# Loads of 16 heads in 16 KB runs, PSUM left in two copies, doubled mixes and transposes in a batched product x·yᵀ on one core

## The chip, the core and the metric

The kernel runs on one core of a Trainium2 chip. Its time is the device time of one launch in microseconds (us). Ten runs of the kernel before have a median of 302.0 us, from 301.79 to 302.33.

## The reference

For each of 8 batches and 12 heads, x and y are 512 x 64 matrices of float32, and the output is their product over the 64 channels, a 512 x 512 matrix of float32:

```python
batch, n_heads, seq_t, seq_s, channels = 8, 12, 512, 512, 64
np.einsum('bhtc,bhsc->bhts', x, y).astype(np.float32)
```

The inputs are 12.6 MB each, the output is 100.7 MB: for each byte read, four are written.

## The kernel before

All 96 heads are taken as one row of heads. A **group** is 8 heads (G); there are 12 (NG). `load` (L73) takes a group's x and y with two DMAs, 1 MB each, into one slot: on each of the 128 partitions 32 consecutive rows of x (8 KB) and 32 of y (8 KB). One pool of five slots of 16 KB per partition (`slots`, L54) serves loads and output tiles alike: an output tile is a slot as well, and `result` fills it before it is stored.

`compress` (L79) empties a slot of inputs: ScalarE casts x to bf16 (`xk`, L83), and the casts of y into `yb` are split in four quarters of 64 partitions: two on VectorE, one on GpSimd, one on ScalarE (`in_front`, L61; the instructions have the line of the helper `copy`, L66 for ScalarE, L68 for the others).

A **pair** `i` is four heads, half a group. `mix` (L99) copies four blocks of 32 partitions of `xk` into a tile `xb` of u32 words, in which one of the two bf16 places of a word stays zero for each half of the channels; two such tiles, one for even and one for odd pairs, are set to zero once (L148 to L150). `transposes` (L113) lets VectorE transpose `xb` and `yb` in blocks of 32 x 32 words into `xT` and `yT`. After that two heads lie one above the other on the 128 partitions of `xT`, with zeros that separate them, and so one matmul with 128 contraction rows makes 64 rows of each of two heads.

`result` (L126) makes output tile `o`, 2 MB: eight matmuls of 128 x 512, into PSUM tiles of 3, 3 and 2 banks (two buffers of 3 banks, one of 2), each copied to the slot by ScalarE, or by VectorE for each fourth tile. Behind that it emits, for later pairs, the transposes or the mixes (VectorE's and ScalarE's in turn). There are 48 output tiles, each stored in 16 KB runs.

The order on each engine is that of the program (`manual_schedule`, L145); engines wait for one another through semaphores alone. All DMAs are issued by SP, in program order, on one queue. The program goes like this: five loads, the zeros, and then for each group `compress`, half of a `mix` by GpSimd, and (L155 to L162) for groups 2 and 4 transposes, for groups 0 to 4 the next load, for groups 5, 7 and 9 an output tile into a slot that is held back, for groups 6 and 8 loads 10 and 11. The three tiles held back are stored after the last load (L163), and then 45 more tiles follow, each made and stored (L165). GpSimd makes the mixes of pairs 0 to 5 in this loop; the later ones come out of `result`.

On ScalarE's queue, for instance, result 0 stands between the casts of groups 5 and 6, result 1 between those of 7 and 8, result 2 between those of 9 and 10. SP issues load 10 when all casts of group 6 have read its slot, and load 11 when those of group 8 have.

Of the kernel before, what the change touches and what calls it, by code (L numbers as in the profile page):

```python
# [1 line left out]

# [4 lines left out]


@with_exitstack
def kernel(  # L10
    ctx: ExitStack,
    tc: tile.TileContext,
    x: bass.AP,
    y: bass.AP,
    out: bass.AP,
):

    nc = tc.nc
    B, H, T, C = x.shape
    _, _, S, _ = y.shape  # L30
    P = 128
    G = 8
    Q = P // G
    R = T // Q
    NG = B * H // G
    K = 8
    E = R // K
    D = 32
    SLOTS = 5
    fp32 = mybir.dt.float32  # L40
    bf16 = mybir.dt.bfloat16
    u32 = mybir.dt.uint32
    COPY = mybir.ActivationFunctionType.Copy
    assert C == 2 * D and S == T and R == D and Q * 2 == D

    xv = x.rearrange("b h t c -> (b h t c)").rearrange("(g p n) -> g p n", p=P, n=R * C)
    yv = y.rearrange("b h t c -> (b h t c)").rearrange("(g p n) -> g p n", p=P, n=R * C)
    ov = out.rearrange("b h t s -> (b h t s)").rearrange(
        "(o u h q n) -> o h q u n", u=2, h=2, q=Q * E, n=K * S
    )  # L50

    const = ctx.enter_context(tc.tile_pool(name="const", bufs=1))
    kept = ctx.enter_context(tc.tile_pool(name="kept", bufs=NG))
    slots = ctx.enter_context(tc.tile_pool(name="slots", bufs=SLOTS))  # L54
    tpool = ctx.enter_context(tc.tile_pool(name="tpool", bufs=3))
    pm3pool = ctx.enter_context(tc.tile_pool(name="pm3psum", bufs=2, space=bass.MemoryType.PSUM))
    pm2pool = ctx.enter_context(tc.tile_pool(name="pm2psum", bufs=1, space=bass.MemoryType.PSUM))

    loaded, inputs, mixed, made = {}, {}, {}, {}
    zeroed = [const.tile([P, K * E * D], u32, name=f"xb{half}") for half in range(2)]  # L60
    in_front = [nc.vector, nc.gpsimd, nc.vector, nc.scalar]  # L61
    FIRST = NG // 2

    def copy(engine, dst, src):
        if engine is nc.scalar:
            nc.scalar.activation(dst, src, COPY)  # L66
        else:
            engine.tensor_copy(dst, src)  # L68

    def slot():  # L70
        return slots.tile([P, K * S], fp32, name="slot")

    def load(g):  # L73
        both = slot()
        nc.sync.dma_start(both[:, :R * C], xv[g])
        nc.sync.dma_start(both[:, R * C:], yv[g])
        loaded[g] = both

    def compress(g):  # L79

        both = loaded.pop(g)
        xk = kept.tile([P, R, C], bf16)
        nc.scalar.activation(xk.rearrange("p r c -> p (r c)"), both[:, :R * C], COPY)  # L83
        inputs[g] = xk
        ys = both[:, R * C:].rearrange("p (r c) -> p r c", c=C)
        for half in range(2):
            yb = kept.tile([P, R // 2 * D], u32, name=f"yb{half}")
            yv2 = yb.bitcast(bf16).rearrange("p (j c w) -> p j w c", j=R // 2, w=2)
            for ch in range(2):
                copy(  # L90
                    in_front[2 * half + ch],
                    yv2[ch * 64:(ch + 1) * 64],
                    ys[half * 64:(half + 1) * 64, :, ch * D:(ch + 1) * D].rearrange(
                        "p (j w) c -> p j w c", w=2
                    ),
                )
            mixed[2 * g + half] = yb

    def mix(i, engines, halves=(0, 1)):  # L99

        g, half = divmod(i, 2)
        xk = inputs[g]
        xv2 = zeroed[half].bitcast(bf16).rearrange("p (k e c u) -> p k e c u", k=K, e=E, u=2)
        for ch in halves:
            for u in range(2):
                lo = half * 64 + u * D
                copy(
                    engines[2 * ch + u],
                    xv2[(2 * ch + u) * D:(2 * ch + u + 1) * D, :, :, :, u],
                    xk[lo:lo + D, :, ch * D:(ch + 1) * D].rearrange("p (e k) c -> p k e c", k=K),  # L110
                )

    def transposes(i):  # L113
        xb, yb = zeroed[i % 2], mixed.pop(i)
        xT = tpool.tile([P, K * D * E], u32)
        nc.vector.transpose(  # L116
            xT.rearrange("p (k r e) -> p k e r", k=K, e=E),
            xb.rearrange("p (k e c) -> p k e c", k=K, e=E),
        )
        yT = tpool.tile([P, D * R // 2], u32)  # L120
        nc.vector.transpose(  # L121
            yT.rearrange("p (r j) -> p j r", r=D), yb.rearrange("p (j c) -> p j c", c=D)
        )
        made[i] = (xT.bitcast(bf16).rearrange("p (k h m) -> p k h m", k=K, h=2), yT.bitcast(bf16))

    def result(o):  # L126

        i, h = divmod(o, 2)
        xT, yT = made[i]
        otf = slot()  # L130
        ot = otf.rearrange("p (r s) -> p r s", s=S)
        for k, n in ((0, 3), (3, 3), (6, 2)):
            pm = (pm3pool if n == 3 else pm2pool).tile([P, n, S], fp32, name=f"pm{n}")
            for j in range(n):
                nc.tensor.matmul(  # L135
                    pm[:, j, :], xT[:, k + j, h, :], yT[:, h * S:(h + 1) * S], start=True, stop=True
                )
            copy(nc.vector if o % 4 == 3 else nc.scalar, ot[:, k:k + n, :], pm)
        if h == 0 and i + 2 < 2 * NG:
            transposes(i + 2)  # L140
        elif h == 1 and FIRST <= i + 4 < 2 * NG:
            mix(i + 4, [nc.scalar if o % 4 == 3 else nc.vector] * 4)
        return lambda: nc.sync.dma_start(ov[i, h], otf)

    with tc.manual_schedule():  # L145
        for g in range(SLOTS):
            load(g)
        for k in range(0, K * E * D, 64):  # L148
            nc.vector.memset(zeroed[0][:, k:k + 64], 0.0)  # L149
            nc.gpsimd.memset(zeroed[1][:, k:k + 64], 0.0)  # L150
        stores = []
        for g in range(NG):
            compress(g)
            mix(g // 2, [nc.gpsimd] * 4, (g % 2,))
            if g in (2, 4):  # L155
                transposes(g // 2 - 1)
            if g < 5:
                load(g + SLOTS)
            elif g in (5, 7, 9):
                stores.append(result(len(stores)))  # L160
            elif g in (6, 8):
                load(g // 2 + 7)  # L162
        for store in stores:  # L163
            store()
        for o in range(len(stores), 4 * NG):  # L165
            result(o)()


# [1 line left out]
_INS = ['x', 'y']  # L170
_OUTS = [((8, 12, 512, 512), 'float32')]


# [23 lines left out]
```

## Time and profile before

| | us |
|---|---|
| median of 10 runs | 302.0 |
| the profiled execution | 301.86 |
| its span, from the first instruction to the last | 300.1 |
| TensorE matmuls busy | 144.5 |
| VectorE busy | 182.6 |
| ScalarE busy | 221.3 |
| GpSimd busy | 59.1 |

The groups of instructions that matter here, as the page lists them (busy us, count, mean ns of one):

| | busy | count | mean ns |
|---|---|---|---|
| ScalarE, PSUM to slot, 1536 elements | 100.8 | 72 | 1452 |
| ScalarE, PSUM to slot, 1024 elements | 37.3 | 36 | 1036 |
| VectorE, PSUM to slot, 1536 elements | 41.0 | 24 | 1751 |
| VectorE, PSUM to slot, 1024 elements | 14.6 | 12 | 1213 |
| VectorE transposes of xb / of yb | 49.1 / 25.3 | 24 / 24 | 2044 / 1056 |
| mixes: GpSimd / ScalarE / VectorE | 38.5 / 48.1 / 26.1 | 24 / 36 / 36 | 1606 / 1336 / 724 |
| y casts: VectorE / GpSimd / ScalarE | 33.8 / 19.2 / 15.9 | 24 / 12 / 12 | 1408 / 1602 / 1328 |
| x casts, ScalarE | 22.9 | 12 | 1910 |

How to read the page: PE is TensorE, DVE VectorE, ACT ScalarE, POOL GpSimd, and SPq the queue of SyncE. The DMA row cuts the span into 40 equal slices of 7.5 us; each digit is the mean busy share of the 16 transfer engines in tenths, 9 for 90% or more. In a timeline a line is: start, duration, engine, line of the code, operation, output and input with their shapes, count; in brackets, how long the engine had been idle before and what ended that. Several like instructions in a row are merged in one line, with the shape of the first. An issue of a DMA shows only the issuing; a transfer's landing is seen in the instruction that it releases.

### The profile page before, as it was taken

The page shows a single profiled execution, that of the slowest core. Times are in us where ns is not written, and L with a number is a line of the kernel's source. Part 1 is how long each engine was busy: PE and PEld are TensorE (multiplying, and loading weights), DVE is VectorE, ACT ScalarE, POOL GpSimd, SP SyncE. Part 2 cuts the span into 40 slices and gives each one's busy share as a digit, 9 for nine tenths or more (in the row PEclk, how much of TensorE's full clock was granted, in tenths as well). Part 3 has the DMA queues.
Part 4 walks back from the last instruction along what each step waited for, and adds up shares of the span by engine and source line. Part 5 has one row for each costly group of instructions (what it writes and reads, how often), then busy time and mean ns, then how long its engine had stood idle before and what let it go on. Part 6 is the DMA issues. An engine that isn't in the chain of part 4 may idle for free.

```text
span 300.1 us, 1419 instructions
## 1 busy us (share of the span) xinstructions
PE 144.5 (48%) x384; PEld 45.9 (15%) x384; DVE 182.6 (61%) x160; ACT 221.3 (74%) x169; POOL 59.1 (20%) x56
## 2 busy tenths in 40 slices
PE   0004044138646465765456657566585557574000
PEld 0001011012212121221112112112121112121000
DVE  1568895979983973937909649288295570603200
ACT  4666599998999869789789697897887977364000
POOL 2899999981000000000000000000000000000000
PEclk9999555557989776677986775857757895776555
DMA  7999999999999999999999999999999999999994
GB/s 289 429 425 422 419 419 426 423 436 431 424 436 430 421 439 430 426 435 430 427 439 426 432 430 428 432 435 426 430 435 428 422 425 435 423 424 430 430 430 210
DMA packets 10377, 125.93 MB, mean 420 GB/s; under 512 B 1152, under 2 KB 1152, under 8 KB 1152
## 3 DMA queue, kind: packets, MB, share of 16 engines
q1 hardware_dynamic: 10368, 125.83, 98.8%
q8 instruction: 3, 0.05, 0.1%
q14 instruction: 6, 0.05, 0.0%
HBM read 25.17 MB, written 100.66 MB: 419 GB/s over the span
## 4 chain that ended last, share of the span: by engine, by line
DMA 53%; ACT 11%; DVE 7%; issue 1%; DVEq 1%; PE 0%; ACTq 0%
DMA out_dram<-slot 53%; ACT slot L66 8%; DVE slot L68 7%; ACT xb L66 2%; ACT xk L83 1%; DVEq L192 1%; PE pm L135 0%; ACT yb L66 0%; DVE yb L68 0%; DVEq L68 0%; ACTq L66 0%
## 5 line engine op out<-in xcount | busy, mean ns | idle before, releaser
L135 PE MATMUL pm<-yT,xT 128*128 128x512 bf16 x384 | 144.5, 514 | 130.7 <-ACT slot L66 75.7
L66 ACT ACTIVATE slot<-pm 128x1536 f32<-128x1536 f32 (+1 forms) x108 | 133.2, 1314 | 37.9 <-DMA out_dram<-slot 28.8
L68 DVE COPY slot<-pm 128x1536 f32<-128x1536 f32 (+1 forms) x36 | 54.6, 1572 | 72.7 <-DMA out_dram<-slot 44.5
L135 PEld LDWEIGHTS <-xT 128*128 128x128 bf16 x384 | 45.9, 120 | 228.4 <-issue 193.4
L116 DVE STREAM_TRANSPOSE xT<-xb 128x1024 uint32<-128x1024 uint32 x24 | 49.1, 2044 | 5.6 <-PE pm L135 4.0
L66 ACT ACTIVATE xb<-xk 32x1024 bf16<-32x1024 bf16 x36 | 48.1, 1336 | 0.9
L68 DVE CAST yb<-slot 64x1024 bf16<-64x1024 f32 x24 | 33.8, 1408 | 17.7 <-DMA slot<-in_y_dram 17.5
L68 POOL COPY xb<-xk 32x1024 bf16<-32x1024 bf16 x24 | 38.5, 1606 | 1.2
L83 ACT ACTIVATE xk<-slot 128x2048 bf16<-128x2048 f32 x12 | 22.9, 1910 | 9.4 <-DMA slot<-in_x_dram 9.3
L68 DVE COPY xb<-xk 32x1024 bf16<-32x1024 bf16 x36 | 26.1, 724 | 0.4
L121 DVE STREAM_TRANSPOSE yT<-yb 128x512 uint32<-128x512 uint32 x24 | 25.3, 1056 | 0.0
L68 POOL CAST yb<-slot 64x1024 bf16<-64x1024 f32 x12 | 19.2, 1602 | 7.5 <-DMA slot<-in_y_dram 6.9
L66 ACT ACTIVATE yb<-slot 64x1024 bf16<-64x1024 f32 x12 | 15.9, 1328 | 3.6 <-DMA slot<-in_y_dram 3.4
L83 ACT ACT_TABLE_LOAD x1 | 1.3, 1283 | 0.7 <-PEq L181 0.7
L149 DVE MEMSET xb<- 128x64 uint32 x16 | 1.2, 112 | 0.8 <-PEq L181 0.8
L150 POOL MEMSET xb<- 128x64 uint32 x16 | 1.4, 151 | 0.3 <-POOLq L181 0.3
L181 POOL MEMSET const-float32-0.0<- 128x1 f32 x1 | 0.1, 98 | 0.2 <-issue 0.2
L181 POOL MEMSET const-float32-1.0<- 128x1 f32 x1 | 0.1, 98 | 0.0
L181 POOL MEMSET const-uint8-127<- 128x1 uint8 x1 | 0.1, 98 | 0.0
L181 POOL MEMSET const-bfloat16-1.0<- 128x1 bf16 x1 | 0.1, 97 | 0.0
## 6 DMA issues: line engine op xcount, KB each, us to landing
out_dram<-slot SPq DMA_DIRECT2D x48, 2048.0 KB, 20.6
slot<-in_x_dram SPq DMA_DIRECT2D x12, 1024.0 KB, 17.5
slot<-in_y_dram SPq DMA_DIRECT2D x12, 1024.0 KB, 19.2
```

The costliest lines, as they stand in the source:

```text
L66: nc.scalar.activation(dst, src, COPY)
L68: engine.tensor_copy(dst, src)
L83: nc.scalar.activation(xk.rearrange("p r c -> p (r c)"), both[:, :R * C], COPY)
L116: nc.vector.transpose(xT.rearrange("p (k r e) -> p k e r", k=K, e=E), xb.rearrange("p (k e c) -> p k e c", k=K, e=E),)
L121: nc.vector.transpose(yT.rearrange("p (r j) -> p j r", r=D), yb.rearrange("p (j c) -> p j c", c=D))
L135: nc.tensor.matmul(pm[:, j, :], xT[:, k + j, h, :], yT[:, h * S:(h + 1) * S], start=True, stop=True)
L149: nc.vector.memset(zeroed[0][:, k:k + 64], 0.0)
L150: nc.gpsimd.memset(zeroed[1][:, k:k + 64], 0.0)
L181: nc = _bacc.Bacc("TRN2", target_bir_lowering=False, num_devices=1)
L192: with _tile.TileContext(nc) as tc:
```

## The change

Groups become 16 heads (G = 16, NG = 6), and a load takes 2 MB of x or of y alone, in runs of 16 KB, with one DMA for one slot. `compress(n)` is now either the cast of x (n even) or those of y (n odd), with twice the elements. A pair becomes eight heads with four output tiles (V = 4), so that mixes and transposes have twice the elements and are half as many. In the loop over the 12 loads GpSimd makes one mix part each (pairs 0 to 2); later, `result` emits transposes and mixes together after a pair's fourth tile, with three parts of a mix on VectorE and one on ScalarE. An output tile leaves PSUM in two copies of four banks. VectorE sets its zeros in 8 parts and GpSimd in 16, that of GpSimd of 128 words. Of the casts' buffers there are NG - 1 instead of NG, of transposed tiles two instead of three.

The order of loads, results held back and stores in the program stays: loads 0 to 4, loads 5 to 9 after `compress` 0 to 4, results after 5, 7 and 9, loads 10 and 11 after 6 and 8. The first transposes stand after `compress(4)`, the second after `compress(8)`. Load 10 now takes the slot of load 6 and load 11 that of load 8, both read by one x cast alone; result 0 takes the slot of load 5, a y.

```diff
--- before.py
+++ after.py
@@ -29,10 +29,12 @@
     B, H, T, C = x.shape
     _, _, S, _ = y.shape
     P = 128
-    G = 8
+    G = 16
     Q = P // G
     R = T // Q
     NG = B * H // G
+    NH = 2 * NG
+    V = G // 4
     K = 8
     E = R // K
     D = 32
@@ -41,25 +43,24 @@
     bf16 = mybir.dt.bfloat16
     u32 = mybir.dt.uint32
     COPY = mybir.ActivationFunctionType.Copy
-    assert C == 2 * D and S == T and R == D and Q * 2 == D
+    assert C == 2 * D and S == T and R == 2 * D and Q * V == D
 
     xv = x.rearrange("b h t c -> (b h t c)").rearrange("(g p n) -> g p n", p=P, n=R * C)
     yv = y.rearrange("b h t c -> (b h t c)").rearrange("(g p n) -> g p n", p=P, n=R * C)
     ov = out.rearrange("b h t s -> (b h t s)").rearrange(
-        "(o u h q n) -> o h q u n", u=2, h=2, q=Q * E, n=K * S
+        "(o u h q n) -> o h q u n", u=2, h=V, q=Q * E, n=K * S
     )
 
     const = ctx.enter_context(tc.tile_pool(name="const", bufs=1))
-    kept = ctx.enter_context(tc.tile_pool(name="kept", bufs=NG))
+    kept = ctx.enter_context(tc.tile_pool(name="kept", bufs=NG - 1))
     slots = ctx.enter_context(tc.tile_pool(name="slots", bufs=SLOTS))
-    tpool = ctx.enter_context(tc.tile_pool(name="tpool", bufs=3))
-    pm3pool = ctx.enter_context(tc.tile_pool(name="pm3psum", bufs=2, space=bass.MemoryType.PSUM))
-    pm2pool = ctx.enter_context(tc.tile_pool(name="pm2psum", bufs=1, space=bass.MemoryType.PSUM))
+    tpool = ctx.enter_context(tc.tile_pool(name="tpool", bufs=2))
+    pmpool = ctx.enter_context(tc.tile_pool(name="pmpsum", bufs=2, space=bass.MemoryType.PSUM))
 
     loaded, inputs, mixed, made = {}, {}, {}, {}
     zeroed = [const.tile([P, K * E * D], u32, name=f"xb{half}") for half in range(2)]
     in_front = [nc.vector, nc.gpsimd, nc.vector, nc.scalar]
-    FIRST = NG // 2
+    FIRST = 3
 
     def copy(engine, dst, src):
         if engine is nc.scalar:
@@ -70,19 +71,20 @@
     def slot():
         return slots.tile([P, K * S], fp32, name="slot")
 
-    def load(g):
-        both = slot()
-        nc.sync.dma_start(both[:, :R * C], xv[g])
-        nc.sync.dma_start(both[:, R * C:], yv[g])
-        loaded[g] = both
+    def load(n):
+        loaded[n] = slot()
+        nc.sync.dma_start(loaded[n], (yv if n % 2 else xv)[n // 2])
 
-    def compress(g):
+    def compress(n):
 
-        both = loaded.pop(g)
-        xk = kept.tile([P, R, C], bf16)
-        nc.scalar.activation(xk.rearrange("p r c -> p (r c)"), both[:, :R * C], COPY)
-        inputs[g] = xk
-        ys = both[:, R * C:].rearrange("p (r c) -> p r c", c=C)
+        src = loaded.pop(n)
+        g = n // 2
+        if n % 2 == 0:
+            xk = kept.tile([P, R, C], bf16)
+            nc.scalar.activation(xk.rearrange("p r c -> p (r c)"), src, COPY)
+            inputs[g] = xk
+            return
+        ys = src.rearrange("p (r c) -> p r c", c=C)
         for half in range(2):
             yb = kept.tile([P, R // 2 * D], u32, name=f"yb{half}")
             yv2 = yb.bitcast(bf16).rearrange("p (j c w) -> p j w c", j=R // 2, w=2)
@@ -96,19 +98,17 @@
                 )
             mixed[2 * g + half] = yb
 
-    def mix(i, engines, halves=(0, 1)):
+    def mix(i, engine, part):
 
         g, half = divmod(i, 2)
-        xk = inputs[g]
+        ch, u = divmod(part, 2)
+        lo = half * 64 + u * D
         xv2 = zeroed[half].bitcast(bf16).rearrange("p (k e c u) -> p k e c u", k=K, e=E, u=2)
-        for ch in halves:
-            for u in range(2):
-                lo = half * 64 + u * D
-                copy(
-                    engines[2 * ch + u],
-                    xv2[(2 * ch + u) * D:(2 * ch + u + 1) * D, :, :, :, u],
-                    xk[lo:lo + D, :, ch * D:(ch + 1) * D].rearrange("p (e k) c -> p k e c", k=K),
-                )
+        copy(
+            engine,
+            xv2[part * D:(part + 1) * D, :, :, :, u],
+            inputs[g][lo:lo + D, :, ch * D:(ch + 1) * D].rearrange("p (e k) c -> p k e c", k=K),
+        )
 
     def transposes(i):
         xb, yb = zeroed[i % 2], mixed.pop(i)
@@ -121,48 +121,50 @@
         nc.vector.transpose(
             yT.rearrange("p (r j) -> p j r", r=D), yb.rearrange("p (j c) -> p j c", c=D)
         )
-        made[i] = (xT.bitcast(bf16).rearrange("p (k h m) -> p k h m", k=K, h=2), yT.bitcast(bf16))
+        made[i] = (xT.bitcast(bf16).rearrange("p (k h m) -> p k h m", k=K, h=V), yT.bitcast(bf16))
 
     def result(o):
 
-        i, h = divmod(o, 2)
+        i, h = divmod(o, V)
         xT, yT = made[i]
         otf = slot()
         ot = otf.rearrange("p (r s) -> p r s", s=S)
-        for k, n in ((0, 3), (3, 3), (6, 2)):
-            pm = (pm3pool if n == 3 else pm2pool).tile([P, n, S], fp32, name=f"pm{n}")
-            for j in range(n):
+        for k in range(0, K, 4):
+            pm = pmpool.tile([P, 4, S], fp32)
+            for j in range(4):
                 nc.tensor.matmul(
                     pm[:, j, :], xT[:, k + j, h, :], yT[:, h * S:(h + 1) * S], start=True, stop=True
                 )
-            copy(nc.vector if o % 4 == 3 else nc.scalar, ot[:, k:k + n, :], pm)
-        if h == 0 and i + 2 < 2 * NG:
-            transposes(i + 2)
-        elif h == 1 and FIRST <= i + 4 < 2 * NG:
-            mix(i + 4, [nc.scalar if o % 4 == 3 else nc.vector] * 4)
+            copy(nc.vector if o % 4 == 3 else nc.scalar, ot[:, k:k + 4, :], pm)
+        if h == V - 1:
+            if i + 2 < NH:
+                transposes(i + 2)
+            if i + FIRST < NH:
+                for part in range(4):
+                    mix(i + FIRST, nc.scalar if part == 3 else nc.vector, part)
         return lambda: nc.sync.dma_start(ov[i, h], otf)
 
     with tc.manual_schedule():
         for g in range(SLOTS):
             load(g)
-        for k in range(0, K * E * D, 64):
-            nc.vector.memset(zeroed[0][:, k:k + 64], 0.0)
-            nc.gpsimd.memset(zeroed[1][:, k:k + 64], 0.0)
+        for half, engine, part in ((0, nc.vector, 256), (1, nc.gpsimd, 128)):
+            for k in range(0, K * E * D, part):
+                engine.memset(zeroed[half][:, k:k + part], 0.0)
         stores = []
-        for g in range(NG):
-            compress(g)
-            mix(g // 2, [nc.gpsimd] * 4, (g % 2,))
-            if g in (2, 4):
-                transposes(g // 2 - 1)
-            if g < 5:
-                load(g + SLOTS)
-            elif g in (5, 7, 9):
+        for n in range(2 * NG):
+            compress(n)
+            mix(n // 4, nc.gpsimd, n % 4)
+            if n in (4, 8):
+                transposes(n // 4 - 1)
+            if n < 5:
+                load(n + SLOTS)
+            elif n in (5, 7, 9):
                 stores.append(result(len(stores)))
-            elif g in (6, 8):
-                load(g // 2 + 7)
+            elif n in (6, 8):
+                load(n // 2 + 7)
         for store in stores:
             store()
-        for o in range(len(stores), 4 * NG):
+        for o in range(len(stores), V * NH):
             result(o)()
 
 
```

## The prediction

> **What bounds the kernel now.** I read the page's slices first, then the timelines of SP, ScalarE, VectorE and GpSimd over the first 80 us, then the chain.
>
> ```profile
> DMA  7999999999999999999999999999999999999994
> q1 hardware_dynamic: 10368, 125.83, 98.8%
> HBM read 25.17 MB, written 100.66 MB: 419 GB/s over the span
> ```
>
> The transfers are busy from the first slice to the last: 125.83 MB go through one queue that never runs dry. So an engine's saving is worth nothing unless the queue is dry somewhere. The question is the opposite: does the change let it run dry? The place where it nearly does is the turn from loads to stores. SP's timeline, and the landings as ScalarE, VectorE and GpSimd show them:
>
> ```profile
> 0.73 0.39 SPq L75 DMA_DIRECT2D slot<-in_x_dram  x1
> 43.81 0.33 SPq L75 DMA_DIRECT2D slot<-in_x_dram  x1
> 54.19 0.33 SPq L75 DMA_DIRECT2D slot<-in_x_dram  x1
> ```
> ```profile
> 7.96 1.32 ACT L66 ACTIVATE yb<-slot 64x1024 bf16<-64x1024 f32 x1 [0.56 <-DMA slot<-in_y_dram]
> 12.95 1.32 ACT L66 ACTIVATE yb<-slot 64x1024 bf16<-64x1024 f32 x1 [0.58 <-DMA slot<-in_y_dram]
> ```
> ```profile
> 52.74 2.48 DVE L68 CAST yb<-slot 64x1024 bf16<-64x1024 f32 x2 [2.47 <-DMA slot<-in_y_dram]
> 63.31 2.48 DVE L68 CAST yb<-slot 64x1024 bf16<-64x1024 f32 x2 [1.75 <-DMA slot<-in_y_dram]
> ```
>
> The first 2 MB are issued at 0.73 and have landed at 7.96; the next 2 MB land 4.98 later. So a load into an idle queue costs 7.23 from its issue: 4.97 of moving and 2.26 fixed. Load 9 lands at 52.74, so load 10 should land at 57.7, and loads 10 and 11, issued at 43.81 and 54.19, had to be issued by 50.5 and 55.4. Load 10 has 6.7 us to spare, load 11 only 1.2. Load 11 lands at 63.31, and the stores follow without a gap until the end. The last time in this stage that matters is therefore the issue of load 11, and ScalarE's queue sets it:
>
> ```profile
> 36.75 3.71 ACT L66 ACTIVATE slot<-pm 128x1536 f32<-128x1536 f32 x3 [2.58 <-DVE yb L68]
> 40.48 1.91 ACT L83 ACTIVATE xk<-slot 128x2048 bf16<-128x2048 f32 x1
> 47.12 3.71 ACT L66 ACTIVATE slot<-pm 128x1536 f32<-128x1536 f32 x3
> 50.85 1.91 ACT L83 ACTIVATE xk<-slot 128x2048 bf16<-128x2048 f32 x1
> 52.79 1.33 ACT L66 ACTIVATE yb<-slot 64x1024 bf16<-64x1024 f32 x1
> ```
>
> From 36.75, when result 0 gets its slot from the VectorE casts of group 5, to 54.12 ScalarE doesn't pause: result 0, groups 6 and 7, result 1, group 8; then load 11's slot is free.
>
> **What the Trainium skill says.** "SBUF — State Buffer", section "Who interferes with whom": VectorE copies in a two-port mode and GpSimd take the same port pair, and the second to issue waits for the first's whole instruction. The trace agrees: the two short ones run alone, the two long ones meet the other engine:
>
> ```profile
> 7.96 0.72 DVE L68 CAST yb<-slot 64x1024 bf16<-64x1024 f32 x1 [5.93 <-DMA slot<-in_y_dram]
> 8.06 1.78 POOL L68 CAST yb<-slot 64x1024 bf16<-64x1024 f32 x1 [5.97 <-DMA slot<-in_y_dram]
> 8.71 1.72 DVE L68 CAST yb<-slot 64x1024 bf16<-64x1024 f32 x1
> 11.66 1.31 POOL L68 COPY xb<-xk 32x1024 bf16<-32x1024 bf16 x1
> ```
>
> A VectorE cast adds 0.47 to a GpSimd instruction; a GpSimd instruction adds 1.0 to a cast. "DMA: Bandwidth & Descriptors", section "Why small descriptors are slow": a packet costs about 3 cycles besides one per 32 B. For 8 KB that is 3 in 259, for 16 KB 3 in 515, an estimate of 0.6% of the loads. "VectorE: DVE Perf Modes", section on the trn2 errata: small instructions pay a fixed time each. The trace agrees: ScalarE's 1452 ns for 1536 elements and 1036 for 1024 leave about 0.2 us fixed.
>
> **The change part by part.** I call a 2 MB load (x or y of 16 heads) by its number n; x is even, y odd.
>
> *Load runs of 16 KB.* The loads go at 2.097 MB per 4.97 us, 422 GB/s; late stores at one per 4.92 (ScalarE released by stores at 265.17 and 270.09). If the loads reach that, 12 x 0.05 = 0.6 us; with 430 from the page's slices 1.1; by the skill's price 0.35; from below, 0. I take 0.5, but it counts only if the queue stays full.
>
> *Two PSUM copies, not three.* By ScalarE's two rows a 2048-element copy is 1.87 us, two are about 3.66 in a row against 3.71; VectorE's 1751 and 1213 give 2.29, two 4.5 against 4.55. Of the 36 and 12 outputs only two are on the path: -0.1. The matmuls now wait for 4 banks instead of 3; the 8 matmuls take 3.63 at the low clock, still inside the 4.92 per output that the stores need.
>
> *Zeros.* 8 VectorE memsets of 256 and 16 GpSimd ones of 128 elements. At 112 and 151 ns for 64 elements, less than 5 us for either, against 7.96 and 11.6 when they have other work: 0. Without this cover: about 2 us.
>
> *Mixes, casts, transposes twice as large.* Half as many instructions, the same elements. After the turn each four outputs (19.7 us) take ScalarE 3 x 3.66 + 2.5 (one mix, 1336 ns doubled less its fixed part) = 13.5, and VectorE 4.5 + 5.4 (transposes) + 3 x 1.3 = 13.7. Both stay hidden beneath the stores, with 6 us to spare. Three buffers become two for the transposed tiles, but a tile is remade only after its four outputs, and the other lasts 4 outputs: 0. The sixth group of casts reuses the first group's buffers, whose last readers (GpSimd's mix 7 at 49, the second transposes at 56) are done before loads 10 and 11 are cast: 0. SP issues 12 loads instead of 24, about 0.4 us each, all beside the moving: 0.
>
> *Where the doubled instructions do count: the path to load 11.* Work starts only when 2 MB of x have landed, instead of 1 MB; four GpSimd mixes and two of its casts must end before the first transposes; VectorE's casts of load 5 stand behind those transposes; result 0 on ScalarE waits for these; and behind result 0 in ScalarE's order is what frees the slots of loads 10 (x cast of load 6) and 11 (x cast of load 8). SP issues in order, so stores 0 to 2 stand behind load 11 too. Step by step:
> - Load 0 lands at 7.9. x cast of 4096 elements: 1.91 + 2048 x 0.833 ns = 3.62 -> 11.6.
> - GpSimd to the end of mix 3: 6 instructions of 2.5 (1.31 doubled less 0.1 fixed), and 4 VectorE casts (loads 1 and 3) at 0.98 each in its way, gaps 0.3: 19.2 -> 30.8. Bounds: two of the casts miss it, 28.9; 2.62 an instruction, 31.5.
> - Transposes: 20.43 to 23.16 is 2.73 for the pair, doubled 5.4 -> 36.3. (The first had come at 20.43 before, the second pair at 30.38.)
> - VectorE casts of load 5 (landed at 32.7): alone 1.26 each. GpSimd, after two instructions since 30.9, began its third at 36.0. The first cast waits for that to end (38.4), the second for the next one (41.9): -> 43.1. If VectorE gets there first, only one is waited for: 40.9. The margin is 0.3 us, so this is nearly a toss; I take the later.
> - ScalarE: result 0 3.66, x cast of load 6 3.64 -> load 10 issued at 50.5; y cast of load 7 2.47, result 1 3.66, x cast of load 8 3.64 -> load 11 issued at 60.4.
>
> Load 10: 50.5 + 7.23 = 57.8, against 57.5 with a full queue (7.96 + 4.95 x 10). Load 11: 60.4 + 7.23 = 67.6. The queue is dry for some 5 us between them. Before, load 11 landed at 63.31: the loads end 4.3 later.
>
> *After it.* Stores 0 and 1 stand ready, store 2 at 66.6. Store 3, on VectorE behind the casts of load 11 (72.4), is ready at 77 and due at 80; store 4 at 81, due at 85. No further gap, and none to win back, because the stores run at the transfers' rate. The 0.5 of the load rate drowns in the gap. Sum: span 300.1 + 4.3 = 304.4; with the 1.76 around it (301.86 - 300.1) 306.2, and as the profiled run lies 0.14 under the median of 302.0, 306.2 to 306.3.
>
> **Rivals.**
> - *VectorE gets the port first* at load 5: the path is 2.2 shorter, load 11 lands at 65.4, +2.1: 304.0. For it: a 0.3 us margin. Against: GpSimd and VectorE leave the same event together, GpSimd's two instructions sum to 5.1, the transposes to 5.4.
> - *No gap: load 11 in time, and the runs bring their gain.* Mechanism: the port isn't contended in front. Without the four blockings GpSimd ends at 26.9, the transposes at 32.3, the casts of load 5 at 36; load 11 is issued at 53.3. It decides at 55.2, which needs the path 5.2 us shorter than my sum. Then the time is 302.0 - 0.5 = 301.5, at best 300.9. Against it: the 1.78 and 1.72 rows show the blocking at each cast.
> - *A later gap too.* Doubled instructions leave VectorE's store 3 only 3 us of cover. If the casts of load 11 each lose a GpSimd instruction more (2 x 2.5), store 3 misses by 2: 308.3; with GpSimd at the upper bound 309.
>
> **How the numbers follow.** The gap as summed (305 to 307.5): 0.50. The shorter one (303 to 305): 0.27. No gap: 0.08, of which 0.05 faster and 0.03 within 0.2%. A later gap or a longer path (307.5 to 310): 0.15. The range 303.0 to 309.0 leaves out the last one's end and the no-gap case. Faster 0.05, within 0.2% (0.6 us, about what a measurement of this kernel can tell from no change) 0.03, slower 0.92.
>
> **What would show it.** In the profile after: slice 7 or 8 of the DMA row at 4 to 7 instead of 9; SP's last load issued near 60 and, between the landings of loads 10 and 11, about 10 us; ScalarE's first PSUM copy near 43 and released by VectorE's cast; GpSimd instructions of about 3.5 where VectorE casts; stores at 4.9 each afterwards. I am wrong if the queue stays full through the turn, or if a gap opens among the stores.

## The result

The changed kernel takes 307.63 us (median of 8 runs, 307.35 to 308.02) against 302.07 (29 runs, 301.7 to 302.33): a ratio of 1.0186, with a 95% interval of 1.0178 to 1.0195, 5.6 us slower. The prediction was 306.2, in a range of 303.0 to 309.0.

The page of the changed kernel, the rows that answer to those of before (40 slices of 7.65 us):

```profile
DMA  7999999499999999999999999999999999999995
GB/s 283 435 426 433 428 428 371 212 317 435 431 428 433 428 433 431 427 433 430 433 426 437 428 433 424 433 432 431 431 426 433 428 431 426 424 433 422 431 426 234
q1 hardware_dynamic: 8640, 125.83, 97.4%
```

Between the first slice and the last one digit is different: the eighth slice, from 53.5 to 61.2, has a 4 where the others have a 9. In three slices (371, 212, 317 GB/s) the rate is low; before and behind them it is as before the change. This stretch is the one in which the transfer engines stand still (the last two columns are their busy share and GB/s):

```profile
58.30:61.60 3.30, 0.44 (x2) 0.14 (x1) 3.29 (x2) 3.28 (x2) 3.19 (x1) 0.98 0.00 0
```

SP's queue there, and the first of the casts that the last load releases:

```profile
50.82 0.33 SPq L76 DMA_DIRECT2D slot<-in_x_dram  x1
60.69 0.33 SPq L76 DMA_DIRECT2D slot<-in_y_dram  x1
61.07 1.67 SPq L145 DMA_DIRECT2D out_dram<-slot  x2
```
```profile
69.50 1.34 DVE L69 CAST yb<-slot 64x2048 bf16<-64x2048 f32 x1 [6.86 <-DMA slot<-in_y_dram]
```

Loads 10 and 11 are issued at 50.82 and 60.69 (forecast: 50.5 and 60.4), and load 11 lands at 69.50 where it had landed at 63.31. Load 10 is late too, by less: from 51 to 54 the rate is 246 GB/s. The queue on ScalarE that sets this, and VectorE's casts ahead of it:

```profile
43.50 3.65 ACT L67 ACTIVATE slot<-pm 128x2048 f32<-128x2048 f32 x2 [7.70 <-DVE yb L69]
47.17 3.62 ACT L84 ACTIVATE xk<-slot 128x4096 bf16<-128x4096 f32 x1
50.81 2.48 ACT L67 ACTIVATE yb<-slot 64x2048 bf16<-64x2048 f32 x1
53.38 3.65 ACT L67 ACTIVATE slot<-pm 128x2048 f32<-128x2048 f32 x2
57.05 3.62 ACT L84 ACTIVATE xk<-slot 128x4096 bf16<-128x4096 f32 x1
```
```profile
23.51 7.82 DVE L69 CAST yb<-slot 64x2048 bf16<-64x2048 f32 x2 [3.98 <-DMA slot<-in_y_dram]
31.37 3.92 DVE L116 STREAM_TRANSPOSE xT<-xb 128x2048 uint32<-128x2048 uint32 x1
35.10 1.94 DVE L121 STREAM_TRANSPOSE yT<-yb 128x1024 uint32<-128x1024 uint32 x1
36.85 13.57 DVE L69 CAST yb<-slot 64x2048 bf16<-64x2048 f32 x4
```

Result 0 starts at 43.50 instead of 36.75 and was released by VectorE's casts; from there ScalarE's queue runs without a pause to the end of the x cast of load 8 at 60.67, and SP issues load 11 at that moment. (The last row merges the casts of loads 5 and 7; those of load 5 take 6.54 us and end at 43.4.) In the kernel before, the casts of the group that result 0 waits for were these:

```profile
33.11 3.52 DVE L68 CAST yb<-slot 64x1024 bf16<-64x1024 f32 x2
```

So of the 6.75 us by which result 0 is late, 3.7 are the later start of the casts (36.85 against 33.11, behind the first transposes, which start at 31.37) and 3.0 their length. Behind result 0 nothing is added: to the end of the casts ahead of the issue ScalarE needs 17.2 us, and needed 17.4.

Span less landing of load 11 is nearly the same in both kernels: 300.1 - 63.31 = 236.8 and 305.9 - 69.50 = 236.4. So the loss lies ahead of that landing, which is 6.2 us later; nothing of it shows behind it, in the 48 stores.

### The profile page after: what moved, and what is told of

The parts are those of the page before. It is cut to its first block, busy times and chain, and to the rows that moved or that the text cites. A ratio compares the mean times of both kernels' runs of the same rounds, so it can differ in the third digit from the quotient of the medians.

```text
span 305.9 us, 1243 instructions
## 1 busy us (share of the span) xinstructions
PE 143.1 (47%) x384; PEld 46.3 (15%) x384; DVE 196.2 (64%) x95; ACT 191.0 (62%) x94; POOL 56.7 (19%) x38
## 3 DMA queue, kind: packets, MB, share of 16 engines
HBM read 25.17 MB, written 100.66 MB: 411 GB/s over the span
## 4 chain that ended last, share of the span: by engine, by line
DMA 54%; ACT 12%; DVE 5%; issue 2%; PE 2%; DVEq 1%; ACTq 0%
DMA out_dram<-slot 51%; ACT slot L67 11%; DVE slot L69 4%; DMA slot<-in_y_dram 3%; PE pm L135 2%; DVE yb L69 2%; ACT xk L84 1%; DVEq L194 1%; DVEq L69 0%; ACTq L67 0%
## 5 line engine op out<-in xcount | busy, mean ns | idle before, releaser
L67 ACT ACTIVATE slot<-pm 128x2048 f32<-128x2048 f32 x72 | 131.0, 1876 | 71.7 <-DMA out_dram<-slot 45.9
L69 DVE COPY slot<-pm 128x2048 f32<-128x2048 f32 x24 | 53.8, 2284 | 66.0 <-DMA out_dram<-slot 65.4
L69 DVE CAST yb<-slot 64x2048 bf16<-64x2048 f32 x12 | 38.5, 3208 | 21.7 <-DMA slot<-in_y_dram 21.5
L116 DVE STREAM_TRANSPOSE xT<-xb 128x2048 uint32<-128x2048 uint32 x12 | 46.7, 3893 | 0.2
L69 POOL COPY xb<-xk 32x2048 bf16<-32x2048 bf16 x12 | 37.3, 3109 | 10.1 <-ACT xk L84 9.5
L69 DVE COPY xb<-xk 32x2048 bf16<-32x2048 bf16 x27 | 35.2, 1303 | 0.3
L84 ACT ACTIVATE xk<-slot 128x4096 bf16<-128x4096 f32 x6 | 21.7, 3617 | 11.8 <-DMA slot<-in_x_dram 11.7
L121 DVE STREAM_TRANSPOSE yT<-yb 128x1024 uint32<-128x1024 uint32 x12 | 23.1, 1921 | 0.0
L67 ACT ACTIVATE xb<-xk 32x2048 bf16<-32x2048 bf16 x9 | 22.2, 2472 | 0.2
L69 POOL CAST yb<-slot 64x2048 bf16<-64x2048 f32 x6 | 16.9, 2818 | 9.3 <-DMA slot<-in_y_dram 9.1
```

The costliest lines, as they stand in the source:

```text
L84: nc.scalar.activation(xk.rearrange("p r c -> p (r c)"), src, COPY)
L116: nc.vector.transpose(xT.rearrange("p (k r e) -> p k e r", k=K, e=E), xb.rearrange("p (k e c) -> p k e c", k=K, e=E),)
L121: nc.vector.transpose(yT.rearrange("p (r j) -> p j r", r=D), yb.rearrange("p (j c) -> p j c", c=D))
```

## The experiments

The theory: the loss is the gap between loads 10 and 11, made by the late issue of load 11, and the path of ScalarE, VectorE and GpSimd to that issue sets it. Rivals: the 16 KB loads themselves cost time; the stores are slower, through PSUM or a later gap; the turn has cover that the sum doesn't know of.

### More on the path: the x cast of load 8 twice

```diff
-            nc.scalar.activation(xk.rearrange("p r c -> p (r c)"), src, COPY)
+            for _ in range(2 if n == 8 else 1):
+                nc.scalar.activation(xk.rearrange("p r c -> p (r c)"), src, COPY)
```

> The changed kernel with the x cast of load 8 done twice in a row on ScalarE (same source, same target), 3.6 us more ahead of the slot that load 11 takes. Theory (ScalarE's queue up to the issue of load 11 sets the end): load 11 issued 3.6 later, near 64.3, and the whole 3.6 us later: 311.2. Rival (the loss lies in the 16 KB loads or in the stores, and the path has some cover left): within 1 us of the changed kernel, 307.6 to 308.6.

Measured: 311.46 us (ratio to the kernel before 1.0308, interval 1.0294 to 1.0322), 3.8 more than the changed kernel. Load 11:

```profile
64.20 0.33 SPq L76 DMA_DIRECT2D slot<-in_y_dram  x1
```

It is issued 3.5 later, and the end is 3.8 later. ScalarE's queue at this place has no cover at all: what was put on it is paid in full.

### Less on the path: two mix parts from GpSimd to ScalarE

```diff
-            mix(n // 4, nc.gpsimd, n % 4)
+            if n == 5:
+                mix(1, nc.scalar, 1)
+                mix(1, nc.scalar, 2)
+            elif n != 6:
+                mix(n // 4, nc.gpsimd, n % 4)
```

> The changed kernel with the second and third part of pair 1's mix moved from GpSimd to ScalarE, both before result 0; GpSimd then has nothing but the y cast while VectorE casts load 5. Theory (GpSimd's mixes hold VectorE's casts of load 5 up by some 4 us): the two casts, 6.65 us in the changed kernel, take 2.6 and end near 39.4; ScalarE, now later with its two mixes, begins result 0 at 40.8 instead of 43.5; load 11 is issued 2.7 earlier and the time is 304.9. Rival (the casts are slow by themselves): casts still over 6 us, result 0 at 43.5 or later, 307.6.

Measured: 304.86 us (1.0094, interval 1.008 to 1.0108). The timelines of VectorE and ScalarE:

```profile
36.55 2.57 DVE L69 CAST yb<-slot 64x2048 bf16<-64x2048 f32 x2
```
```profile
35.54 4.98 ACT L67 ACTIVATE xb<-xk 32x2048 bf16<-32x2048 bf16 x2
40.55 3.65 ACT L67 ACTIVATE slot<-pm 128x2048 f32<-128x2048 f32 x2
```
```profile
57.72 0.33 SPq L76 DMA_DIRECT2D slot<-in_y_dram  x1
```

The same two casts take 2.57 us without GpSimd's mixes beside them and 6.54 with them. So 4.0 us of the path were waiting for GpSimd's instructions, now twice as long. Load 11 is issued 3.0 earlier. ScalarE got 4.98 us more work and the kernel became 2.8 faster, because that work filled a wait.

### The gap taken away: results 0 and 1 one place later

Results 0 and 1 are emitted behind loads 10 and 11. The slots change hands with that: load 10 takes the slot of load 5, load 11 that of load 7, and the results those of loads 6 and 8. (The diff is cut: `result` now takes its slot as an argument.)

```diff
-            elif n in (5, 7, 9):
+            elif n in (5, 7):
+                held = slot()
+            elif n == 9:
                 stores.append(result(len(stores)))
             elif n in (6, 8):
                 load(n // 2 + 7)
+                stores.append(result(len(stores), held))
```

> The changed kernel with results 0 and 1 each emitted one place later: behind the cast of load 6 or 8 and behind the issue of load 10 or 11. Load 10 then takes the slot of load 5 and load 11 that of load 7. Theory: load 10 issued near 43.5, load 11 near 50.5, both before the queue is dry; the gap of 5 us goes, load 11 lands at 62.6 to 63.2, and with loads at 4.89 each the time is 300.7 to 301.6, under the kernel before. Rival (run length or stores cost the time): the gap goes but the time stays above 305.

Measured: 301.24 us, a ratio of 0.9971 to the kernel before, interval 0.9959 to 0.9982. The page and SP's timeline:

```profile
DMA  7999999999999999999999999999999999999995
```
```profile
43.23 0.33 SPq L76 DMA_DIRECT2D slot<-in_x_dram  x1
50.23 0.33 SPq L76 DMA_DIRECT2D slot<-in_y_dram  x1
50.60 5.01 SPq L145 DMA_DIRECT2D out_dram<-slot  x2
```

The 4 has become a 9, load 11 is issued 10.5 earlier than in the changed kernel and lands at 62.53, and the time falls by 6.4. That load 11 has the slot of load 7 is seen in its issue at 50.23: the x cast of load 8 ends only at 51.32. All the rest of the change is still in this kernel: larger runs, two PSUM copies, doubled mixes, casts and transposes. Together they cost no time that shows, and the whole is 0.9 us faster than the kernel before in the same runs (302.13).

### What the run length is worth

The version without the gap, with each load in two DMAs of 1 MB in runs of 8 KB:

```diff
-        nc.sync.dma_start(loaded[n], (yv if n % 2 else xv)[n // 2])
+        src = (yv if n % 2 else xv)[n // 2]
+        for part in range(2):
+            cols = slice(part * R * C // 2, (part + 1) * R * C // 2)
+            nc.sync.dma_start(loaded[n][:, cols], src[:, cols])
```

> The kernel without the gap (results 0 and 1 one place later), but each load in two DMAs of 1 MB in runs of 8 KB. This prices the run length where the queue never runs dry: with 4.97 instead of 4.89 for each 2 MB, 12 loads cost 1.0 us more: 301.9 to 302.4. Rival (run length worth nothing, the gain of the version without the gap comes from elsewhere): 301.0 to 301.4.

Measured: 302.25 us (1.0008, interval 0.9999 to 1.0016), 1.0 more than with 16 KB runs. The stretch from 10 to 50 us of the two versions, with the rate as last column and the DMA share ahead of it, 16 KB first:

```profile
10.00:50.00 40.00, 7.20 (x16) 2.37 (x17) 32.53 (x10) 28.76 (x11) 36.41 (x13) 1.00 1.01 431
```
```profile
10.00:50.00 40.00, 7.21 (x16) 2.33 (x17) 33.55 (x10) 29.48 (x11) 35.96 (x12) 1.00 1.01 424
```

431 against 424 GB/s while both queues are full: over 25.17 MB that is 59.4 - 58.4 = 1.0 us, as much as the times differ. The profiled executions spread it: load 11 lands 0.6 later (63.15 against 62.53), 0.2 more lie between there and the end of the span, and 0.2 outside the span (302.29 - 300.3 against 301.25 - 299.5). With 8 KB runs the version without the gap can't be told from the kernel before, so its gain goes with the longer runs, and the rest of the change costs 0.5 us at most by the interval. (12 DMAs more go together with the shorter runs; no run has the two apart.)

### The changed kernel with runs of 8 KB

The same edit on the changed kernel, to see whether the long runs made its loads land late.

> The changed kernel with each load of 2 MB made by two DMAs of 1 MB in runs of 8 KB, all else the same. Measured so far: in the changed kernel load 0 lands 0.9 later than the same 2 MB in the kernel before, and load 11 8.8 after its issue, not 7.2. If runs of 16 KB into an idle queue are the reason: load 0 lands near 8.0 and load 11 7.2 to 7.8 after its issue, loads go at 4.97 instead of 4.89, and the time is 305.2 to 306.2. If the run length isn't the reason: load 0 near 8.8, and 307.6 to 308.6.

Measured: 309.25 us (1.0239, interval 1.0223 to 1.0255): neither of the two cases, 1.6 slower than the changed kernel. One reason is seen on ScalarE:

```profile
8.24 1.28 ACT L87 ACT_TABLE_LOAD   x1 [8.24 <-DMA slot<-in_x_dram]
9.54 3.62 ACT L87 ACTIVATE xk<-slot 128x4096 bf16<-128x4096 f32 x1
```

With two DMAs for the first x, the table load of 1.28 us stands behind the wait for them instead of ahead of it, and the first x cast starts at 9.54, not 8.84. The whole path is later by that: load 11 is issued at 61.35 and lands at 70.09. So this run doesn't isolate the run length. Load 0 does land earlier, at 8.24 and not 8.84. But the question on load 11 is answered: it lands 8.74 after its issue with 8 KB runs and 8.81 with 16 KB. The long runs are not the reason for its late landing. Of the remaining 1 us, 0.6 lie behind load 11's landing (237.0 against 236.4) and 0.2 outside the span; what makes them stays open.

### Stores behind the last load

```diff
-        for store in stores:
-            store()
+        for k in (2, 0, 1):
+            stores[k]()
```

> The changed kernel with the three held stores issued in the order 2, 0, 1. Store 2 is ready only at 66.9, so no store stands right behind load 11, which is issued at 60.7 as before. If stores close behind a load slow its last packets: load 11 lands 68.0 to 68.9 instead of 69.5. If a load into a dry queue costs 8.8 by itself: 69.5. The time is 307 to 309.5 either way, since the queue can run dry again before store 2.

Measured: 308.57 us (1.0217, interval 1.0198 to 1.0235). Load 11 is issued at 60.39 and lands here:

```profile
68.49 4.77 DVE L69 CAST yb<-slot 64x2048 bf16<-64x2048 f32 x2 [6.19 <-DMA slot<-in_y_dram]
```

8.10 after its issue, against 8.81 with stores right behind it (8.56 to 8.81 in the four versions of the changed kernel that have the gap and the stores behind it). So the stores that follow closely made the load's end 0.5 to 0.7 later, by one execution of each. The other 8.1 belong to a load into a dry queue.

### The same gap in the kernel before

```diff
-        nc.scalar.activation(xk.rearrange("p r c -> p (r c)"), both[:, :R * C], COPY)
+        for _ in range(3 if g == 8 else 1):
+            nc.scalar.activation(xk.rearrange("p r c -> p (r c)"), both[:, :R * C], COPY)
```

> The kernel before with the x cast of group 8 done three times, 3.85 us more on ScalarE ahead of the slot of load 11, so that load 11 is issued near 58.0, with 8 KB runs and none of the change. The cover was worked out as 1.2 us. By the price of 7.23 for a load into a dry queue load 11 lands at 65.3 and the time is 304.1; by 8.8, as in the changed kernel, 66.8 and 305.6. Rival (the turn has more cover, and the gap isn't made by a late issue): within 0.5 of 302.0.

Measured: 305.8 us (1.0126, interval 1.0112 to 1.014). Issue and landing:

```profile
58.19 0.33 SPq L75 DMA_DIRECT2D slot<-in_x_dram  x1
58.57 0.42 SPq L76 DMA_DIRECT2D slot<-in_y_dram  x1
```
```profile
67.34 2.48 DVE L68 CAST yb<-slot 64x1024 bf16<-64x1024 f32 x2 [5.67 <-DMA slot<-in_y_dram]
```

The kernel before, with nothing of the change in it, loses 3.75 us (from 302.05) by the late issue alone. Load 11 lands 9.15 after the issue of its x and 8.77 after that of its y, as in the changed kernel. So the gap needs neither long runs nor doubled instructions, only 4 us more ahead of one DMA issue.

The loss is larger than the time in which the transfer engines stand still:

```profile
57.40:59.10 1.70, 0.00 (x0) 0.00 (x0) 1.70 (x3) 1.68 (x2) 1.63 (x2) 0.50 0.00 0
59.10:67.30 8.20, 3.63 (x8) 1.11 (x8) 2.56 (x2) 8.05 (x7) 3.65 (x3) 0.51 0.98 321
```

They stand still for 1.7 us, and then, up to the landing, they are busy but move 321 GB/s, where the kernel before has 431 from 53 to 67. Over 8.2 us that is another 2.1, an estimate. The changed kernel has the same: 346 GB/s from 61.6 to 69.5, which makes 1.6. So behind the pause of the queue 1.6 to 2.1 us more are lost; why the rate is low there, no run shows. With the cover of 1.2 us that the prediction had read, and a loss of one for one beyond it, an issue 4.0 us later would have cost 2.8. Smaller delays were not tried, so where the loss begins stays open.

### The PSUM part alone

The three PSUM tiles of an output become two of four banks, in the kernel before. (The diff is cut: the two pools become one.)

```diff
-        for k, n in ((0, 3), (3, 3), (6, 2)):
-            pm = (pm3pool if n == 3 else pm2pool).tile([P, n, S], fp32, name=f"pm{n}")
+        for k, n in ((0, 4), (4, 4)):
+            pm = pmpool.tile([P, n, S], fp32)
```

> The kernel before with only the PSUM part of the change: two tiles of 4 banks, two copies of 2048 elements for each output. Theory: nothing, 301.8 to 302.4, because the stores are fed by transfers at their own rate and ScalarE gains 0.06 an output that nobody waits for. Rival (matmuls that must wait for 4 banks at once hold up the copies): slower by 1 us or more.

Measured: 301.93 us (0.9992, interval 0.9984 to 1.0). The groups of copies, busy us and mean ns ahead of the idle time:

```profile
L65 ACT ACTIVATE slot<-pm 128x2048 f32<-128x2048 f32 x72 | 131.1, 1876 | 39.8 <-DMA out_dram<-slot 30.5 <-PE pm L134 5.0 <-DVE yb L67 2.6
L67 DVE COPY slot<-pm 128x2048 f32<-128x2048 f32 x24 | 53.8, 2283 | 71.6 <-DMA out_dram<-slot 50.4 <-issue 19.6 <-PE pm L134 1.6
```

1876 and 2283 ns a copy, as worked out (1870 and 2290). The row of ScalarE in the kernel before:

```profile
L66 ACT ACTIVATE slot<-pm 128x1536 f32<-128x1536 f32 (+1 forms) x108 | 133.2, 1314 | 37.9 <-DMA out_dram<-slot 28.8
```

No effect that the interval tells from none: the 2.1 us that ScalarE gains (133.2 to 131.1) become idle time (37.9 to 39.8), most of it waiting for stores.

### All runs together

| | load 11 issued | landed | landing after issue | span | span less landing |
|---|---|---|---|---|---|
| kernel before | 54.19 | 63.31 | 9.12 (queue full) | 300.1 | 236.8 |
| results one place later | 50.23 | 62.53 | 12.30 (queue full) | 299.5 | 237.0 |
| the same, runs of 8 KB | 51.39 | 63.15 | 11.76 (queue full) | 300.3 | 237.1 |
| kernel before, two PSUM copies | 54.19 | 62.88 | 8.69 (queue full) | 300.2 | 237.3 |
| mixes on ScalarE | 57.72 | 66.46 | 8.74 | 303.1 | 236.6 |
| kernel before, late load | 58.19 | 67.34 | 9.15 | 303.9 | 236.6 |
| changed kernel | 60.69 | 69.50 | 8.81 | 305.9 | 236.4 |
| changed kernel, runs of 8 KB | 61.35 | 70.09 | 8.74 | 307.1 | 237.0 |
| x cast twice | 64.20 | 72.76 | 8.56 | 309.5 | 236.7 |

A landing is the start of the first cast that waits for load 11, on VectorE or, where VectorE is busy then, on GpSimd. Nine kernels whose spans are 10 us apart have the same last column, to 0.9 us. The landing of load 11 explains the spans to that accuracy. Only the kernel with store 2 first is off it (306.8 - 68.49 = 238.3): its transfers thin out a second time before store 2, to 262 GB/s from 67 to 68.

## Why the prediction was right, and what was off

The mechanism held: the late issue of load 11 opens one gap, the waits that were named make the issue late, and the likeliest case came about. The time lies 1.4 us above the likeliest value. In the order of the steps:

- *Landing of load 0*: 7.9 forecast, 8.84 measured; other kernels here with the same loads had 8.49 to 8.71. A miss of 0.6 to 0.9, of which 0.3 are left at the issue of load 11, because the next steps came out a little shorter than forecast. That is luck.
- *x cast*: 3.62, as forecast. *GpSimd's six instructions*: from 12.52 to 30.18, 17.7 against 19.2. They are not what the first transposes wait for: VectorE's own casts of load 3, held up by GpSimd (7.82 us for the two), end at 31.33, and the transposes follow without a pause. The sum had only GpSimd's end in this place (30.8), and so was nearly right with the wrong engine last. *Transposes*: 5.5 against 5.4.
- *VectorE's casts of load 5*: 6.54 against 6.8, with GpSimd first, the case that was taken in a near toss, and so in part luck. GpSimd's third instruction starts at 36.30 by its timeline, VectorE's cast at 36.85, a margin of 0.55 where 0.3 was forecast. The run with two mixes on ScalarE shows the wait itself: 4.0 us of the 6.54.
- *ScalarE from result 0 to the issue of load 11*: 43.50 to 60.69, 17.2 as summed (43.1 to 60.4 in the forecast).
- *Landing of load 11*: this term was mis-sized. The prediction added 7.23 us, the landing of the first 2 MB after their issue in the kernel before; measured were 8.81. It is 1.6 of the 1.9 us by which load 11 lands later than forecast (69.50 against 67.6). The runs show 8.1 for a dry queue without stores behind the load, and 0.5 to 0.7 for the stores. The 7.23 was a load with more loads behind it, in two DMAs of 8 KB runs, at the start of the kernel. The cover of 1.2 us came out of the same 7.23, and the run with the late load doesn't bear it out one for one.
- *After load 11*: no further gap, as forecast; store 3 was copied by 78.6 instead of 77 and still came in time. The rival of a later gap didn't come about.
- *PSUM copies*: forecast as 0.1 us less on the path, too little to tell (301.93 against 302.13). *Zeros*: forecast as nothing. No run has them alone; VectorE's last one ends at 3.0 by its timeline, with the first cast at 13.72.
- *Run length*: forecast as 0.5 us, lost in the gap. Measured where the queue is full: 1.0, of which 0.6 are at the landing of load 11. It was indeed lost in the changed kernel, whose queue moves 432 GB/s up to the gap and then waits.

The rival without a gap needed the path 5.2 us shorter, by casts that GpSimd doesn't hold up; the 6.54 us speak against that. With the other order of two results and two loads the time does lie at 301.24, near where that rival had put it (301.5), but by another way: the casts of load 5 still take 6.57 us there. The price for packets that the prediction took from the Trainium skill ("DMA: Bandwidth & Descriptors", section "Why small descriptors are slow (HBM only)"; an estimate of 0.35 us) was below the 1.0 measured. What it took from "SBUF — State Buffer", section "Who interferes with whom", that of a VectorE copy in a two-port mode and a GpSimd instruction the second waits for the whole of the first, agrees with the 2.57 against 6.54; that a shared port is the reason, no trace shows.

## What to carry to other kernels

In a kernel that its transfers bound, look for the DMA issue with the least time to spare, and follow what stands ahead of it in every engine's order; here it was one issue, and 4 us more ahead of it were enough for the loss. Doubling the size of instructions hardly changes their own work (VectorE's transposes are busy 69.8 us in all, and were 74.4), but an engine that waits for one of them waits longer, and a load's slot comes free later. What frees a slot for the next load belongs ahead of work that is needed later: here one place in the order was worth 6.4 us. And a queue that ran dry cost more than its pause: here 1.6 to 2.1 us more, by the estimate above.

## What the runs showed of the hardware that was not expected

A 2 MB load in runs of 16 KB into a dry queue lands 7.8 to 8.1 us after its issue (load 0, and load 11 with store 2 first), where loads in a full queue follow one another every 4.89, and where the first 2 MB of the kernel before took 7.23; with stores issued right behind it, 8.6 to 8.8. In the changed kernel the 16 transfer engines finish load 0 between 7.58 and 8.81 by their semaphores, and the spread of 1.2 us stays in the loads that follow, up to load 9; in the kernel before they finish the first y between 7.63 and 7.94. So the first engine is as early in both, and what makes the load land late is the last one. After a pause of the queue the transfer engines are busy and yet move only 321 to 346 GB/s up to the landing of the load. Between 10 and 50 us loads in runs of 16 KB move at 430 to 432 GB/s and in runs of 8 KB at 423 to 424, in five kernels of 16 KB and five of 8 KB.
